# Two-layer hybrid encoder trunk on one core: trace durations in the planner, two KK and two TT tiles, independent key moves, x in four transfers

## The chip, the core and the metric

The kernel runs on one core of one Trainium2 chip. A core has a matrix engine (TensorE, PE), three engines for element-wise work (VectorE, DVE; ScalarE, ACT; GpSimd, POOL), a queue engine (SyncE, SP) that issues transfers here, and 16 DMA engines. The engines run side by side, each through its own list of instructions in order, and wait for each other by semaphores. Products go into PSUM, where one bank holds 128 x 512 float32; all else lives in SBUF. The metric is the device time of one execution in microseconds, lower is better.

## The reference

Two layers over x of 512 tokens x 1024 channels, all float32. `c` is one vector per sequence that gives six modulation vectors per layer.

```
for l in range(DEPTH):
    mod = cond @ w_ada[l] + b_ada[l];  sh1, sc1, g1, sh2, sc2, g2 = split(mod, 6)
    h = rmsnorm(x, norm1_w[l]) * (1 + sc1) + sh1
    x = x + g1 * token_mixers(h, ...)
    h = rmsnorm(x, norm2_w[l]) * (1 + sc2) + sh2
    x = x + g2 * conv_ffn(h, ...)
return rmsnorm(x, final_norm_w)

def token_mixers(h, ...):
    a_val, a_gate, q_att, k_att, v_att, q_rec, z_fwd, z_bwd, i_rec, g_rec = split(h @ w_in)
    a   = silu(layernorm(conv31(a_val * sigmoid(a_gate))))             # 256 channels
    att = mixture over 3 dilated windows of softmax attention, 6 heads # 384 channels
    rec = rmsnorm(hgrn2 forward + hgrn2 backward) * silu(g_rec)        # 384 channels, 6 heads
    return concat(a, att, rec) @ w_out

def hgrn2_gate(z, lb):
    f = lb + (1 - lb) * sigmoid(z);   k = (1 - lb) * sigmoid(-z)

def conv_ffn(h, ...):
    gate, val = split(conv3(h @ w_up));   return (gelu(gate) * val) @ w_down
```

## The kernel before

x is kept transposed, as eight tiles of 128 channels x 512 tokens, and all activations likewise. A float32 factor is split into a high part that TensorE's fast fp32r form takes whole and a low part (hi, lo), and a product is three fp32r products, high by high, high by low and low by high (`block`). Weights come from HBM in chunks of 128 rows by up to 1024 columns (tag `wr`), one chunk being one column tile over all eight row tiles; the `splitter` thread makes `wh` and `wl` of it. One column tile of w_in is thus 24 products of 512 columns into one PSUM bank (tag `g`, two banks; `m`, four, and `m2` serve all small products).

A layer's mixers begin with six column tiles at once (`FIRST`, whose h arrives tile by tile), then 22 one after the other (`REST`). As soon as a column tile is done, an `evac` thread takes it out of its bank: sigmoids for gates, high and low parts for attention's q and k, copies for values. When all tiles of a pair of heads are there, `evac` starts `rec` (the recurrence, in seven levels of small products) or `att` (attention: scores, masks, exponentials, transposes of P, products with V), and `conv` runs 31 steps on VectorE. The tiles that concern the change: `KK` and `TT` hold the two directions' key gates and decay of one pair of recurrence heads, from the read-out of the gate column Z_F to the end of that pair's `rec`. There was one of each, so `evac` of the next pair's Z_F waits for both (`"KK", "TT"` in its first yield), and its bank waits with it. Z_B of the same pair waits until Z_F has taken the tiles.

Attention's key tile needs each head's 64 rows twice, as high and low part. Head 0's tile and head 1's tile keep high and low part in different halves of the partitions, and transfers within SBUF (`shift`, line 275, issued on SP's queue) move 64 rows to the other half. For keys there were three transfers: two from tile 0 into tile 1, and one within tile 0 that overwrites rows which the other two still read, and so has to wait until both have landed.

What sets the order: nothing is scheduled on the chip. When the program is built, Python runs the threads with a model of the engines' clocks (`Clock`). Every issued operation gets a cost in us (line 160 on for the element-wise engines, `mm`, `transpose`, `dma` and `shift` for the others), and `run_threads` always continues the thread of the highest priority whose needs are met at the model's present time. The order in which operations are written is the order in which each engine runs them. So a number such as `CP` (the priority of conv, 2.5, behind recurrence's 1.0 and attention's 2.0; lower goes first) or the price of a product changes which instruction stands ahead of which. The times of the model are used for nothing else.

The start (`start`): x comes in eight transfers and then `par` (all small parameters), w_ada and w_sh tiles and the first weights, all on SP's queue. `stats` squares x on ScalarE, adds two squares on VectorE, and sums over channels on TensorE with 128x1 products, four pairs in turn; then root and reciprocal, a spread over the partitions, and `mods` makes h of it. `shifts` and `scales` make the first modulation vectors.

All operations of VectorE and ScalarE are issued by one helper and carry its line, L181; matmuls carry L284 and transposes L290. Names in the profile are tile names without buffer numbers.

Of the kernel before, what the change touches and what calls it, by code (L numbers as in the profile page):

```python
# [19 lines left out]
T = 512  # L20
# [20 lines left out]

BUFFERS = dict(wr=(4, 5), wh=(4, 4), wl=(4, 4), hx=(4, 8), qk=(4, 3), PT=(4, 4), KK=(4, 1), QQ=(4, 1), S=(4, 1),
               TT=(6, 1), ao=(2, 2), vr=(2, 2), va=(2, 1), bias=(4, 2), wa=(4, 1), tmp=(2, 5), P=(2, 2), sc=(1, 1),
               ap=(4.25, 1), acc=(2, 2), sm=(0.03125, 8), km=(2, 1), gs=(2, 3), qr=(2, 2), t2=(2, 2))
# [148 lines left out]
class Kernel:  # L193
# [79 lines left out]
    def shift(self, out, in_):  # L273

        self.nc.sync.dma_start(out=out.bitcast(F32), in_=in_.bitcast(F32))
        c = self.clk
        t = max(c.t.get("DMA", 0.0), c.t["PE"], c.written(in_) or 0.0) + size(in_) * in_.shape[0] * 4 / 350e3
        c.t["DMA"] = t
        lo, hi = span(out)
        c.w.setdefault(out.tensor.name, []).append((lo, hi, t + 2.4, "DMA"))  # L280
        c.last[out.tensor.name] = t + 2.4

    def mm(self, out, lhsT, rhs, start, stop, **kw):
        self.nc.tensor.matmul(out, lhsT=lhsT, rhs=rhs, start=start, stop=stop, **kw)  # L284
        n, m = size(out), out.shape[0]
        c = 0.009 + n * 0.000408 if rhs.dtype == F32R else n * 0.00168 * {32: 0.5, 64: 0.51}.get(m, 1.0)
        self.clk.issue("PE", c, [out], [lhsT, rhs])

    def transpose(self, out, in_):
        self.nc.tensor.transpose(out, in_, self.ident)  # L290
        self.clk.issue("PE", 0.109, [out], [in_])

# [75 lines left out]
    def splitter(self):  # L368
        for i in range(len(self.chunks)):
            more = MTAG + ["bias", "wa", "ap"] if i in self.wide else []  # L370
            yield (lambda: 0.0 if i in self.raw and i <= self.cur_chunk + (WA if i in self.wide else 3) else None,)
            t = self.raw.pop(i)
            yield (t, [["wh"] + more, 1], [["wl"] + more, 1])
            hi = self.sb([128, 1024], ["wh"] + more, F32R)[:, :t.shape[1]]
            self.copy(hi, t)
            yield (hi, DM, [["wl"] + more, 1])
            lo = self.sb([128, 1024], ["wl"] + more, F32R)[:, :t.shape[1]]
            self.v.tensor_tensor(out=lo, in0=t, in1=hi.bitcast(F32), op=ALU.subtract)
            self.give(t)
            self.wt[i] = (hi, lo)  # L380
# [49 lines left out]
    def setup(self):  # L430
# [6 lines left out]

        self.x = [one.tile([128, T], F32, name=f"x{k}") for k in range(KD)]
        self.par = one.tile([128, NPAR], F32, name="par")
# [15 lines left out]
    def bounds(self):  # L455

        g = self.par[:, P_GAM:P_GAM + 12].rearrange("p (l j) -> p l j", l=2)
        yield (self.par, lambda: self.clk.written(self.h[KD - 1]))
        lw = self.one.tile([128, 3, 6], F32, name="lw")
# [284 lines left out]
    def start(self):  # L744
# [10 lines left out]

        for k in range(KD):
            self.dma(self.x[k], a["xT"][:, k])
        self.dma(self.par, a["par"])
        for k in range(3):
            load_ada(k)  # L760
            self.loaded.add(k)
            self.load_chunk(k)
        acc = self.sb([128, T], "t2")
        halves = [slice(0, H2), slice(H2, T)]
# [19 lines left out]
        def stats():  # L784
            ps = self.pst("m")
            old = None
            for k in range(KD):
# [7 lines left out]
                v.tensor_tensor(out=sq, in0=sq, in1=old, op=ALU.add)  # L795
                self.give(old)
                yield (sq,)
                self.mean_sq(ps, [sq], slice(0, T), k == 1, k == KD - 1)
                self.give(sq)
                if k == 3:  # L800
                    for i in range(2):
                        v.tensor_copy(self.cb[:, i * 512:i * 512 + 512], cps[i].rearrange("p k c -> p (k c)"))
                    self.give(diag, *cps)
            self.preload(AF.Sqrt)
            d = yield from self.roots(ps, slice(0, T))
            self.give(ps)
            ready.append(1)
            self.spawn(scales(), 0.4)
            yield (lambda: 0.0 if len(ready) > 1 else None,)
# [8 lines left out]
        def scales():  # L818
            for k in range(KD):
                yield (lambda: 0.0 if k in self.sc else None,)  # L820
                yield (self.sc[k], self.cb, SM)
                self.ada_tile(0, 8 + k, self.sc.pop(k))
# [80 lines left out]
    def evac(self, l, n, ps):  # L903
# [51 lines left out]
        elif n >= Q_ATT:  # L955
# [16 lines left out]
            else:  # L972

                yield (ps, ["qk", 2])
                t = [self.sb([128, 2, T], "qk", F32R) for _ in range(2)]
                self.copy(t[0][:, 0], ps)
                yield (t[0][:, 0], DM)
                v.tensor_tensor(out=t[0][:, 1], in0=ps, in1=t[0][:, 0].bitcast(F32), op=ALU.subtract)
                self.give(ps)
                yield (t[0],)  # L980
                for hd in range(2):
                    self.shift(t[1][own[hd]], t[0][own[1]])
                self.shift(t[0][own[1]], t[0][own[0]])
            cur["qa" if q else "ka", p] = t
# [484 lines left out]
```

## Time and profile before

| | us |
|---|---|
| three runs | 1365.31, 1365.95, 1364.5 |
| their median | 1365.31 |
| the profiled execution's own time | 1367.1 |
| its span on the core | 1365.3 |

The profile shows one execution, whose own time is 1.8 us above the median; the span is what the profiler saw of it, from the first to the last instruction. The page gives busy time by engine, the chain of work that ended last, and groups of instructions. Windows give busy times in stretches of the span; the column PEclk there is the mean clock that TensorE was granted, as a share of full speed. Busy time of TensorE is modelled at its ends, since products are pipelined: a busy TensorE is one with work in it and not always one at its peak. A row of waits names who waited, for whose tile, total us, times, and the longest.

### The profile page before, as it was taken

How to read it: one execution, taken by the hardware profiler on the slowest of the kernel's cores; microseconds unless marked ns; L12 is line 12 of the kernel's file. 1: busy time of each engine (PE TensorE's matmuls, PEld its weight loads, DVE VectorE, ACT ScalarE, POOL GpSimd, SP SyncE). 2: the span in 40 equal slices, each digit the busy share in tenths (PEclk: the TensorE clock that was granted, in tenths of full speed). 3: DMA queues.
4: the chain of work that ended last, by engine and by line, in shares of the span. 5: the costliest groups of instructions: out<-in, count | busy, mean ns of one | idle time of the engine just before them, and what ended most of it. 6: DMA issues, size and time to landing. Idle time of an engine off the chain costs nothing.

```text
span 1365.3 us, 24377 instructions
## 1 busy us (share of the span) xinstructions
PE 1328.6 (97%) x9936; PEld 1103.7 (81%) x9936; DVE 1060.7 (78%) x1820; ACT 611.2 (45%) x1024; POOL 2.1 (0%) x16
## 2 busy tenths in 40 slices
PE   8998999999999999999999999999899999999997
PEld 7976777779988888888898786777798888888887
DVE  6898889987698999666785998888667565666666
ACT  5535548574442333233453473758445232333332
POOL 0000000000000000000000000000000000000000
PEclk9999999999999999999999999999999999999998
DMA  9645353342358787421612413114221423233221
GB/s 360 214 147 160 121 170 109 106 122 96 122 157 318 221 289 250 140 100 47 193 49 80 133 62 112 34 48 145 92 76 48 139 64 107 85 105 119 62 78 63
DMA packets 57664, 175.48 MB, mean 129 GB/s; under 512 B 6736, under 2 KB 8784, under 8 KB 57552
## 3 DMA queue, kind: packets, MB, share of 16 engines
q1 hardware_dynamic: 57552, 173.92, 39.7%
q8 instruction: 78, 1.28, 0.4%
q14 instruction: 34, 0.28, 0.1%
HBM read 165.50 MB, written 2.10 MB: 123 GB/s over the span
## 4 chain that ended last, share of the span: by engine, by line
PE 79%; DVE 13%; DMA 4%; ACT 2%; issue 2%; SPq 0%; DVEq 0%; ACTq 0%
PE m L284 52%; PE g L284 25%; DVE acc L181 2%; DMA qk<-qk 2%; DVE wl L181 2%; PE m L290 2%; DVE QQ L181 1%; DVE KK L181 1%; DVE P L181 1%; DVE tmp L181 1%; DVE TT L181 1%; DVE wa L181 1%; ACT P L181 1%; DVE x L181 1%; ACT wh L181 0%
## 5 line engine op out<-in xcount | busy, mean ns | idle before, releaser
L284 PE MATMUL g<-hx,wh 128*128 128x512 f32 (+1 forms) x1280 | 402.7, 391 | 0.5 <-DVE qr L181 0.3
L284 PE MATMUL m<-hx,wh 128*128 128x512 f32 (+1 forms) x1152 | 324.4, 365 | 1.1 <-DVE hx L181 1.1
L284 PEld LDWEIGHTS g<-hx,wh 128*128 128x128 f32 x1280 | 235.4, 189 | 49.2 <-issue 3.9
L181 DVE TENSOR_TENSOR wl<-wr,wh 128x1024 fp32r<-128x1024 f32 (+3 forms) x212 | 217.5, 1028 | 69.7 <-ACT wh L181 63.8
L181 ACT CAST wh<-wr 128x1024 fp32r<-128x1024 f32 (+3 forms) x174 | 154.8, 891 | 236.4 <-PE m L284 161.6
L284 PE MATMUL g<-hx,wl 128*128 128x512 f32 (+1 forms) x636 | 248.1, 390 | 0.0
L284 PEld LDWEIGHTS m<-hx,wh 128*128 128x128 f32 x1152 | 207.7, 189 | 36.5 <-DVE hx L181 1.7
L284 PE MATMUL m<-hx,wl 128*128 128x512 f32 (+1 forms) x584 | 211.2, 362 | 0.0
L284 PEld LDWEIGHTS g<-hx,wl 128*128 128x128 f32 x636 | 119.9, 188 | 22.6 <-issue 0.2
L284 PEld LDWEIGHTS m<-hx,wl 128*128 128x128 f32 x584 | 110.2, 189 | 16.8
L181 DVE SCALAR_TENSOR_TENSOR x<-m,mod,x 128x256 f32<-128x256 f32 (+1 forms) x112 | 66.3, 593 | 43.0 <-PE m L284 42.4
L181 DVE SCALAR_TENSOR_TENSOR acc<-ap,par,acc 128x512 f32<-128x512 f32 x120 | 89.7, 747 | 2.1
L181 DVE SCALAR_TENSOR_TENSOR tmp<-m,par,tmp 128x511 f32<-128x511 f32 x120 | 89.3, 747 | 2.0
L181 ACT ACTIVATE P<-P,sm 128x512 f32<-128x512 f32 x78 | 56.2, 723 | 49.5 <-DVE sm L181 49.3
L181 DVE CAST wh<-wr 128x1024 fp32r<-128x1024 f32 (+3 forms) x42 | 25.3, 603 | 51.8 <-PE m L284 38.3
L181 ACT ACT_TABLE_LOAD x49 | 62.9, 1283 | 4.9 <-DVE tmp L181 3.3
L181 ACT ACTIVATE tmp<-tmp 128x512 f32<-128x512 f32 x44 | 27.8, 633 | 77.2 <-DVE tmp L181 77.2
L181 ACT COPY km<-KK 128x512 f32<-128x512 f32 x30 | 20.6, 685 | 82.5 <-DVE KK L181 59.2
L181 DVE CUSTOM_DVE_ANT_0 wa<-wa,cb,par 128x1024 f32<-128x1024 f32 x40 | 51.1, 1279 | 7.1 <-DMA wa<-w_ada 7.0
L181 ACT ACTIVATE tmp<-m,par 128x512 f32<-128x512 f32 x60 | 40.6, 685 | 31.1 <-PE m L284 28.9
L181 DVE CUSTOM_DVE_ANT_0 bias<-bias,cb,par 128x1024 f32<-128x1024 f32 x39 | 49.6, 1279 | 1.6 <-DMA bias<-w_ada 1.6
L181 DVE SCALAR_TENSOR_TENSOR tmp<-g,par,tmp 128x511 f32<-128x511 f32 x56 | 41.8, 747 | 10.5 <-ACT tmp L181 9.5
(310 smaller groups left out, 2097.5 us busy)
## 6 DMA issues: line engine op xcount, KB each, us to landing
wr<-w_up SPq DMA_DIRECT2D x76, 512.0 KB, 3.5
wr<-w_in SPq DMA_DIRECT2D x44, 512.0 KB, 3.9
wa<-w_ada SPq DMA_DIRECT2D x40, 512.0 KB, 3.9
bias<-w_ada SPq DMA_DIRECT2D x39, 512.0 KB, 4.5
wr<-w_down SPq DMA_DIRECT2D x32, 320.0 KB, 3.0
wr<-w_down SPq DMA_DIRECT2D x32, 256.0 KB, 2.6
wr<-w_in SPq DMA_DIRECT2D x16, 384.0 KB, 5.7
wr<-w_up SPq DMA_DIRECT2D x16, 384.0 KB, 3.1
```

Source lines behind the costliest of these rows:

```text
L181: r = f(*a, **k)
L284: self.nc.tensor.matmul(out, lhsT=lhsT, rhs=rhs, start=start, stop=stop, **kw)
L290: self.nc.tensor.transpose(out, in_, self.ident)
```

## The change

- `KK` and `TT` get two tiles each, `wr` three instead of five.
- `CP` goes from 2.5 to 1.5: conv stands between recurrence (1.0) and attention (2.0).
- The planner's costs: fp32r products 0.0135 + n x 0.000417 us, other fp32 products by their shape, 0.1 us for each change of TensorE's tile shape (`SWITCH`), and 4.5 instead of 2.4 us from the issue of a key or query move to its landing.
- The key tile: two ScalarE copies of the bank give both heads' high parts, VectorE makes the low part, ScalarE copies it to the second tile, and then each tile has one transfer of its own, within itself.
- The start: x is one tile and comes in four transfers of two row tiles; the first 56 columns of `par` come ahead of it and the rest after the first weights; four squares are added on VectorE before they are summed on TensorE; the root's table is loaded earlier; the products of constants that `first_group` put ahead of the first real one are not in the list any more; the splitter waits for the root.

```
-BUFFERS = dict(wr=(4, 5), ..., KK=(4, 1), QQ=(4, 1), S=(4, 1),
-               TT=(6, 1), ...
+BUFFERS = dict(wr=(4, 3), ..., KK=(4, 2), QQ=(4, 1), S=(4, 1),
+               TT=(6, 2), ...
-CP = 2.5
+CP = 1.5
+SWITCH = 0.1
...
     def shift(self, out, in_):
-        c.w.setdefault(out.tensor.name, []).append((lo, hi, t + 2.4, "DMA"))
-        c.last[out.tensor.name] = t + 2.4
+        l = c.w.setdefault(out.tensor.name, [])
+        l[:] = [e for e in l if not (lo <= e[0] and e[1] <= hi)] + [(lo, hi, t + 4.5, "DMA")]
+        c.last[out.tensor.name] = c.last[in_.tensor.name] = t + 4.5
...
     def mm(self, out, lhsT, rhs, start, stop, **kw):
-        c = 0.009 + n * 0.000408 if rhs.dtype == F32R else n * 0.00168 * {32: 0.5, 64: 0.51}.get(m, 1.0)
-        self.clk.issue("PE", c, [out], [lhsT, rhs])
+        mode = (lhsT.shape[0], m)
+        if rhs.dtype == F32R:
+            c = 0.0135 + n * 0.000417
+        elif mode == (128, 128):
+            c = max(0.22 if n == 1 else 0.17, n * 0.00168 + 0.005)
+        else:
+            c = {(64, 32): 0.016, (128, 32): 0.027}.get(mode, n * 0.00086)
+        self.clk.issue("PE", c + (SWITCH if mode != self.mode else 0.0), [out], [lhsT, rhs])
+        self.mode = mode
...
     def splitter(self):
-            yield (lambda: 0.0 if i in self.raw and i <= ...
+            yield (lambda: 0.0 if self.rooted and i in self.raw
...
     def start(self):
-        for k in range(KD):
-            self.dma(self.x[k], a["xT"][:, k])
-        self.dma(self.par, a["par"])
+        self.dma(self.par[:, :P_CW], a["par"][:, :P_CW])
+        for k in range(0, KD, 2):
+            self.dma(self.xall[:, k:k + 2], a["xT"][:, k:k + 2])
         for k in range(3):
             load_ada(k)
             self.loaded.add(k)
             self.load_chunk(k)
+            if k == 0:
+                self.dma(self.par[:, P_CW:], a["par"][:, P_CW:])
...
         def stats():
                 v.tensor_tensor(out=sq, in0=sq, in1=old, op=ALU.add)
                 self.give(old)
+                if k % 4 == 1:
+                    pair = sq
+                    continue
+                yield (sq, pair)
+                v.tensor_tensor(out=sq, in0=sq, in1=pair, op=ALU.add)
+                self.give(pair)
+                if k == KD - 1:
+                    self.spawn(scales(), 0.4)
                 yield (sq,)
-                self.mean_sq(ps, [sq], slice(0, T), k == 1, k == KD - 1)
+                self.mean_sq(ps, [sq], slice(0, T), k == 3, k == KD - 1)
...
     def evac(self, l, n, ps):
                 t = [self.sb([128, 2, T], "qk", F32R) for _ in range(2)]
-                self.copy(t[0][:, 0], ps)
+                for hd in range(2):
+                    self.s.copy(t[hd][:, 0], ps)
                 yield (t[0][:, 0], DM)
                 v.tensor_tensor(out=t[0][:, 1], in0=ps, in1=t[0][:, 0].bitcast(F32), op=ALU.subtract)
                 self.give(ps)
-                yield (t[0],)
+                yield (t[0][:, 1],)
+                self.s.copy(t[1][:, 1], t[0][:, 1].bitcast(F32))
+                yield (t[1],)
                 for hd in range(2):
-                    self.shift(t[1][own[hd]], t[0][own[1]])
-                self.shift(t[0][own[1]], t[0][own[0]])
+                    self.shift(t[hd][own[1 - hd]], t[hd][own[hd]])
```

The order that the planner writes changes throughout; three places follow. In the rows `<-` stands between output and inputs, names carry the number of their buffer, and `xN` means N in a row.

The first is ScalarE in layer 0, where the gate columns of the second recurrence pair are read out of their banks (`KK<-g`, with the other sigmoid `tmp<-g`), amid the attention of the first pair (`P`). Before:

```order
L181 ACTIVATE P_226_1633,sm_228_1635<-P_226_1633,sm_227_1634 128x512
L181 CAST wh_230_1647<-wr_162_1203 128x1024
L181 ACTIVATE P_233_1658,sm_235_1660<-P_233_1658,sm_234_1659 128x512
L181 COPY st_157<-tmp_224_1618 64x3x64 x2
L181 ACT_TABLE_LOAD
L181 ACTIVATE tmp_236_1667<-g_184_1428 128x512
L181 ACTIVATE KK_237_1668<-g_184_1428 128x512
L181 ACTIVATE tmp_239_1672<-g_214_1564 128x512
L181 ACTIVATE KK_237_1668<-g_214_1564 128x512
```

With the change:

```order
L182 CAST wh_196_1494<-wr_169_1247 128x1024
L182 ACTIVATE tmp_198_1498<-g_182_1403 128x512
L182 ACTIVATE KK_199_1499<-g_182_1403 128x512
L182 COPY tmp_205_1517<-m_204_1513 128x384
L182 COPY tmp_207_1523<-m_206_1519 128x384
L182 ACT_TABLE_LOAD
L182 ACTIVATE P_208_1526,sm_210_1528<-P_208_1526,sm_209_1527 128x512
L182 ACTIVATE P_211_1531,sm_213_1533<-P_211_1531,sm_212_1532 128x512
L182 COPY tmp_217_1554<-m_216_1544 128x64
```

Before, the two read-outs stand together, behind the first pair's exponentials and a table load. Now the first of them stands ahead of those exponentials.

The second is SP's queue in layer 0, where the first key tile's moves stand (L275 before, L276 now; `qk<-tmp` is the query's). Before:

```order
L263 DMA wa_171_1281<-w_sh 128x1024
L275 DMA qk_165_1211<-tmp_166_1212 64x512 x2
L263 DMA wr_178_1347<-w_in 128x1024
L275 DMA qk_174_1289<-qk_173_1288 64x1024 x2
L275 DMA qk_173_1288<-qk_173_1288 64x1024
L263 DMA wa_182_1418<-w_ada 128x1024
L263 DMA bias_186_1432<-bias 128x896
L263 DMA bias_187_1433<-bias 128x896
```

With the change:

```order
L264 DMA wr_169_1247<-w_in 128x1024
L276 DMA qk_163_1188<-tmp_164_1189 64x512 x2
L264 DMA wa_178_1334<-w_ada 128x1024
L264 DMA wr_179_1339<-w_in 128x1024
L276 DMA qk_174_1310<-qk_174_1310 64x1024
L276 DMA qk_175_1311<-qk_175_1311 64x1024
L264 DMA bias_184_1413<-bias 128x896
L264 DMA bias_185_1414<-bias 128x896
```

Three key moves, one of which reads and writes the tile that the others read, have become two that each stay within one tile; right behind them stand the bias loads, where a wa load stood first.

The third is TensorE in the start, from the sums over channels (`m<-onesD,tmp`, 128x1) to the first product of h (`g<-hx`). Before:

```order
L284 MATMUL m_23_225<-onesD,tmp_25_228 128x1 x4
L284 MATMUL m_23_225<-onesD,tmp_29_241 128x1 x4
L284 MATMUL m_23_225<-onesD,tmp_31_252 128x1 x4
L284 MATMUL m_23_225<-onesD,tmp_33_261 128x1 x4
L284 MATMUL m_0_36_279<-PT_2_177,sc_19_202 32x128 x8
L284 MATMUL g_37_288<-tmp_35_272,onesD 128x256 x2
L284 MATMUL m_0_36_279<-mean_145,km_42_300 128x1
L284 MATMUL g_43_304<-onesC,onesD 128x128 x4
L284 MATMUL m_0_52_326<-PT_5_183,sc_19_202 32x128 x8
L284 MATMUL g_43_304<-hx_11_194,wh_40_296 128x256 x2
```

With the change:

```order
L286 MATMUL m_23_215<-onesD,tmp_27_223 128x1 x4
L286 MATMUL m_0_32_247<-PT_2_166,sc_19_192 32x128 x8
L286 MATMUL m_23_215<-onesD,tmp_31_241 128x1 x4
L286 MATMUL m_0_32_247<-mean_138,km_36_265 128x1
L286 MATMUL g_38_276<-tmp_37_271,onesD 128x256 x2
L286 MATMUL m_0_43_291<-PT_5_173,sc_19_192 32x128 x8
L286 MATMUL g_47_307<-hx_11_184,wh_39_277 128x256 x2
```

Four groups of sums have become two; the first shifts (`m<-PT,sc`) stand between them and not behind, and the products of `onesC` by `onesD` are gone.

More of the change, by code (lines that the diff above doesn't have):

```diff
@@ L39 @@
 H2 = T // 2
-BUFFERS = dict(wr=(4, 5), wh=(4, 4), wl=(4, 4), hx=(4, 8), qk=(4, 3), PT=(4, 4), KK=(4, 1), QQ=(4, 1), S=(4, 1),
-               TT=(6, 1), ao=(2, 2), vr=(2, 2), va=(2, 1), bias=(4, 2), wa=(4, 1), tmp=(2, 5), P=(2, 2), sc=(1, 1),
+BUFFERS = dict(wr=(4, 3), wh=(4, 4), wl=(4, 4), hx=(4, 8), qk=(4, 3), PT=(4, 4), KK=(4, 2), QQ=(4, 1), S=(4, 1),
+               TT=(6, 2), ao=(2, 2), vr=(2, 2), va=(2, 1), bias=(4, 2), wa=(4, 1), tmp=(2, 5), P=(2, 2), sc=(1, 1),
                ap=(4.25, 1), acc=(2, 2), sm=(0.03125, 8), km=(2, 1), gs=(2, 3), qr=(2, 2), t2=(2, 2))
@@ L285, in mm @@
         n, m = size(out), out.shape[0]
-        c = 0.009 + n * 0.000408 if rhs.dtype == F32R else n * 0.00168 * {32: 0.5, 64: 0.51}.get(m, 1.0)
-        self.clk.issue("PE", c, [out], [lhsT, rhs])
+        mode = (lhsT.shape[0], m)
[7 more added lines that the diff above has]
+        self.mode = mode
     def transpose(self, out, in_):
         self.nc.tensor.transpose(out, in_, self.ident)
-        self.clk.issue("PE", 0.109, [out], [in_])
+        self.clk.issue("PE", 0.109 + (SWITCH if self.mode != (128, 128) else 0.0), [out], [in_])
+        self.mode = (128, 128)
     def spawn(self, gen, prio, slack=0.0):
@@ L370, in splitter @@
             more = MTAG + ["bias", "wa", "ap"] if i in self.wide else []
-            yield (lambda: 0.0 if i in self.raw and i <= self.cur_chunk + (WA if i in self.wide else 3) else None,)
+            yield (lambda: 0.0 if self.rooted and i in self.raw
+                   and i <= self.cur_chunk + (WA if i in self.wide else 3) else None,)
             t = self.raw.pop(i)
@@ L436, in const @@
             return t
-        self.x = [one.tile([128, T], F32, name=f"x{k}") for k in range(KD)]
+        self.xall = one.tile([128, KD, T], F32, name="x")
+        self.x = [self.xall[:, k] for k in range(KD)]
         self.par = one.tile([128, NPAR], F32, name="par")
@@ L457, in bounds @@
         g = self.par[:, P_GAM:P_GAM + 12].rearrange("p (l j) -> p l j", l=2)
-        yield (self.par, lambda: self.clk.written(self.h[KD - 1]))
+        yield (self.par[:, P_CW:], lambda: self.clk.written(self.h[KD - 1]))
         lw = self.one.tile([128, 3, 6], F32, name="lw")
@@ L532 @@
     critical = False
+    rooted = False
+    mode = (128, 128)
     def ada_thread(self, l, order, tags, margin, every=0.0):
@@ L796, in stats @@
                 self.give(old)
+                if k % 4 == 1:
[6 more added lines that the diff above has]
+                    self.spawn(scales(), 0.4)
                 yield (sq,)
-                self.mean_sq(ps, [sq], slice(0, T), k == 1, k == KD - 1)
+                self.mean_sq(ps, [sq], slice(0, T), k == 3, k == KD - 1)
                 self.give(sq)
                 if k == 3:
+                    self.preload(AF.Sqrt)
                     for i in range(2):
@@ L803, in stats @@
                     self.give(diag, *cps)
-            self.preload(AF.Sqrt)
             d = yield from self.roots(ps, slice(0, T))
+            self.rooted = True
             self.give(ps)
             ready.append(1)
-            self.spawn(scales(), 0.4)
             yield (lambda: 0.0 if len(ready) > 1 else None,)
@@ L820, in scales @@
                 yield (lambda: 0.0 if k in self.sc else None,)
-                yield (self.sc[k], self.cb, SM)
+                yield (self.sc[k], self.cb, SM) + ((self.h[0][:, 1, :H2],) if k == 1 else ())
                 self.ada_tile(0, 8 + k, self.sc.pop(k))
```

## The prediction

> **What bounds the kernel now.** I read first the page's shares and chain of waits, then the busy times by stage, then, only in the stages where TensorE (PE) isn't always busy, its waits and the rows around them. The page's line 1 and the chain:
>
> ```profile
> PE 1328.6 (97%) x9936; PEld 1103.7 (81%) x9936; DVE 1060.7 (78%) x1820; ACT 611.2 (45%) x1024; POOL 2.1 (0%) x16
> ...
> PE 79%; DVE 13%; DMA 4%; ACT 2%; issue 2%; SPq 0%; DVEq 0%; ACTq 0%
> ```
>
> TensorE is the bound, so only what it loses can be won. The windows say where it loses (columns: stretch, its length, then busy time and count of PE, weight loads, VectorE (DVE), ScalarE (ACT), POOL, then granted clock, DMA share, GB/s). The stretches shown are the start, layer 0's mixers after their first products, with the out projection, layer 0's gated MLP, layer 1's mixers and its MLP:
>
> ```profile
> 0.00:22.00 22.00, 17.15 (x94) 15.14 (x94) 12.39 (x32) 10.24 (x19) 1.76 (x12) 1.00 0.91 334
> ...
> 63.00:312.00 249.00, 237.28 (x2688) 180.46 (x2687) 222.40 (x427) 146.38 (x268) 0.18 (x2) 0.98 0.42 130
> 312.00:735.00 423.00, 422.14 (x2210) 364.24 (x2209) 335.88 (x528) 163.77 (x252) 0.18 (x2) 1.00 0.50 164
> 735.00:968.00 233.00, 222.87 (x2578) 172.64 (x2578) 201.53 (x386) 135.93 (x240) 0.00 (x0) 0.99 0.29 86
> 968.00:1331.00 363.00, 362.66 (x1776) 307.84 (x1776) 232.91 (x327) 127.87 (x190) 0.00 (x0) 1.00 0.29 89
> ```
>
> The MLPs have nothing to give (422.14 of 423, 362.66 of 363). The mixers of layer 0 leave TensorE idle for 249.00 - 237.28 = 11.7 us, those of layer 1 for 233.00 - 222.87 = 10.1. The clock column hides a second loss, which narrower windows show:
>
> ```profile
> 131.90:138.70 6.80, 6.80 (x29) 6.36 (x29) 4.38 (x11) 5.84 (x9) 0.00 (x0) 0.50 0.45 145
> 189.90:193.30 3.40, 3.40 (x73) 2.59 (x72) 2.67 (x4) 0.00 (x0) 0.00 (x0) 0.50 0.92 310
> 961.30:964.70 3.40, 3.13 (x9) 1.98 (x11) 0.95 (x2) 1.37 (x4) 0.00 (x0) 0.50 0.38 120
> ```
>
> At clock 0.50, half of these windows is lost: 3.4, 1.7 and 1.7 us. So the mixers can give at most 11.7 + 10.1 + 6.8 = 28.6 us, 2% of the kernel. What follows asks which part of that the change reaches.
>
> **KK and TT doubled.** The rows of TensorE and then of ScalarE around 130 us:
>
> ```profile
> 126.05 0.39 PE L284 MATMUL g<-hx,wl 128*128 128x512 f32 x1
> 127.81 0.63 PE L290 MATMUL m<-ident,P 128*128 128x128 f32 x4 [1.37 <-DVE P L181]
> 130.88 0.66 PE L290 MATMUL m<-ident,P 128*128 128x128 f32 x4 [1.98 <-DVE P L181]
> 137.90 1.00 PE L284 MATMUL g<-hx,wh 128*128 128x512 f32 x2
> ...
> 133.00 0.60 ACT L181 ACTIVATE tmp<-g 128x512 f32<-128x512 f32 x1
> 133.49 0.59 ACT L181 ACTIVATE KK<-g 128x512 f32<-128x512 f32 x1
> 133.97 0.60 ACT L181 ACTIVATE tmp<-g 128x512 f32<-128x512 f32 x1
> 134.44 0.62 ACT L181 ACTIVATE KK<-g 128x512 f32<-128x512 f32 x1
> 126.40:137.90 11.50, 8.15 (x42) 7.51 (x41) 9.74 (x27) 9.21 (x16) 0.00 (x0) 0.74 0.34 104
> ```
>
> Both "g" banks hold gate columns of the second recurrence pair (Z_F+1 and Z_B+1), which ScalarE reads only at 133.0 to 135.1, when the first pair has given KK and TT back. From 126.4 to 137.9 no column product (g<-hx) is issued: TensorE lives on the attention's small transposes, which wait for VectorE. Idle is 11.50 - 8.15 = 3.35 us, and the first cold window lies here. With a second KK and TT the read-out stands right behind the product in ScalarE's order, ahead of the exponentials (first pair of order rows above). That is worth 3.35 + 3.4 = **6.75 us**; at least 0, if a bank is still held for another reason. [...]
>
> **Key moves.** A key tile was copied, its low part taken, two transfers issued, and a third that had to wait for the first two:
>
> ```profile
> 180.07 0.47 SPq L275
> 180.59 5.42 DMA qk<-qk
> 186.07 2.93 DMA qk<-qk
> SPq L275 <- DMA qk<-qk: 13.5, 3, 5.2
> SPq L275 <- DMA qk<-qk: 10.5, 3, 4.5
> PE m L284 <- DMA qk<-qk: 6.0, 5, 2.0
> DVE wa L181 <- DMA wa<-w_ada: 3.0, 1, 3.0
> DVE wa L181 <- DMA wa<-w_ada: 2.7, 1, 2.7
> 97.43 0.58 ACT L181 CAST qk<-g 128x512 fp32r<-128x512 f32 x1
> ```
>
> (The two SPq wait rows are of 60 to 312 and 735 to 972 us, the two wa rows of 63 to 130 and 130 to 200.) Now two transfers go out at once, after two more ScalarE copies. One stands ahead of the subtraction beside work that was there; the other, of the low part, is new on the path: 0.58 us. Saved per move: 0.5 of issue + 2.93 - 0.58 = 2.8 us, and the longest of TensorE's five waits is 2.0. So all **6.0 us** go (2.7 in layer 0, 3.4 in layer 1, by the same view of each stage), and the cold 1.7 at 189.9, which follows the wait that ends at 189.0. If the new order asks for the keys earlier, 3.4 remain as the low end. SP's queue was blocked for 5.2 us behind the third transfer, and the wa load queued there came late for VectorE: 3.0 + 2.7 = 5.7 us of VectorE's waits go too, in a stage where it has little to spare.
>
> **The end of layer 1's mixers.** TensorE's longest wait there:
>
> ```profile
> PE m L290 <- ACT P L181: 3.4, 1, 3.4
> 374.73 10.88 PE g L284 x48
> ```
>
> It is the last attention pair's transposes at some 960 us, with the third cold window behind. In the changed order that pair's last tiles stand about three weight chunks of the out projection, 36 products, earlier. At 10.88 / 48 = 0.227 us that is 8.2 us of cover for a wait of 3.4: 3.4 + 1.7 = **5.1 us** (0 if the pair arrives later by as much).
>
> **What it adds.** VectorE: over the program five casts and two tensor-tensors more, nearly all in layer 0's mixers.
>
> ```profile
> L181 DVE CAST wh<-wr 128x1024 fp32r<-128x1024 f32 (+3 forms) x42 | 25.3, 603 | 51.8 <-PE m L284 38.3
> 11.65 0.69 DVE L181 TENSOR_TENSOR tmp<-tmp,tmp 128x512 f32<-128x512 f32 x1 [0.65 <-ACT tmp L181]
> L181 ACT ACT_TABLE_LOAD x49 | 62.9, 1283 | 4.9 <-DVE tmp L181 3.3
> 131.70 1.28 ACT L181 ACT_TABLE_LOAD   x1
> DVE P L181 <- PE m L290: 3.0, 1, 3.0
> ```
>
> 5 x 0.603 + 2 x 0.69 = 4.4 us, so VectorE would be busy for 222.4 + 4.4 = 226.8 us of that stage. TensorE's own time there becomes 249 - 3.35 - 3.4 - 2.7 - 1.7 = 237.9. But VectorE was idle for 26.6 us, and I can name 5.7 (late loads) and 3.0 (the wait for the transposes of the stall at 130 us, last row) that go; if all else stays, it ends at 226.8 + 17.9 = 244.7. I take the middle, **241** (-8). Ends: 237.9 (-11.1), and 247.7 (-1.3) if only the late loads go.
>
> ScalarE: seven table loads more, 7 x 1.283 = 9.0 us, since exponentials and gate sigmoids now alternate, and some 7 casts more, 7 x 0.58 = 4.1. It is idle for over 95 us in either mixer stage (249 - 146.4, 233 - 135.9), so most is hidden; I count one load in the path of a read-out, **+1.5**, ends 0 and +9.0. [...]
>
> wr falls from five buffers to three. A load took 3.9 us (the page's wr<-w_in), and three buffers still start it two or more chunks ahead, of 24 products or 5.4 us each: 0, at worst +5 if one burst of loads comes late. The dearer fp32 prices, the price of a tile-mode change and conv's new rank act only through the order, which I read as it is.
>
> **The start.**
>
> ```profile
> 9.65 1.97 ACT L181 ACTIVATE tmp<-x 128x512 f32<-128x512 f32 x3 [1.01 <-DMA x<-xT]
> 11.06 3.57 PE L284 MATMUL m<-onesD,tmp 128*128 128x1 f32 x16 [0.39 <-DVE tmp L181]
> 14.56 1.10 PE L284 MATMUL m<-PT,sc 128*32 128x128 f32 x16
> 19.07 2.05 PE L284 MATMUL g<-onesC,onesD 128*128 128x128 f32 x8
> 22.08 0.58 PE L284 MATMUL g<-hx,wh 128*128 128x256 f32 x1
> ```
>
> The last sums end at 14.63; half as many are 1.8 us less, less one more addition of 0.69. But the 1.10 us of shift products stand now ahead of the last sums, and the eight filler products before the first real one are gone, so the first real ones may run at half clock. I take **-1**, ends -3 (sums and par's shorter transfer in full) and +2 (up to 3.4 us cold, 1.7, and some of the shift).
>
> **Sum**, against the profiled execution's own 1367.1 us (span 1365.3): layer 0's mixers -8, layer 1's -8.5 (3.4 + 5.1), ScalarE +1.5, start -1: -16, so 1351.1. That execution is 1.8 above the median of the runs, 1365.31; on the median's scale 1349.3, **forecast 1349**.
>
> **Rivals.** (1) VectorE sets layer 0: the gates are read early, but the recurrences behind them are VectorE's, and the stage ends at 247.7. For it: 222.4 busy of 249, more work. Against: its waits at 126 to 134 us are part of the same knot. Then -1.3 - 8.5 + 1.5 - 1 = -9.3: 1356. Chance 0.2.
> (2) A new gap, cold. In the changed order layer 0's last column products come sooner than VectorE's mixed outputs, so TensorE can run dry where the out projection begins, for VectorE's lag of 244.7 - 237.9 = 6.8 us; at half clock after it another 1.7 to 3.4 go. [...] Layer 0 then gets 249 - 237.9 - 6.8 - 3.4 = 0.9: -0.9 - 8.5 + 1.5 - 1 = -8.9, or 1356.5. Chance 0.13.
> (3) Slower: ScalarE's in-order queue. If all seven loads (9.0) stand in the chain from gate read-out through recurrence to attention, VectorE's 4.4 come on top, and the banks are held as long as before (read-outs behind loads instead of behind KK), only the waits for keys return, 6.0 + 1.7: +5.7, 1371. It decides once more than 3.3 us of loads, three of seven, lie on that chain while the banks and layer 1's end give nothing. For it: exponentials and sigmoids are interleaved in the order rows. Against: ScalarE is at 59% in that stage. Chance 0.13.
> (4) Nothing but the named waits goes wrong and the stalls I left alone (11.7 - 6.05 in layer 0, 10.1 - 6.8 in layer 1: 9 us) shrink too: 1340. Chance 0.1.
>
> **How the numbers follow.** The forecast has 0.44; its own range is 1343 to 1356. 1336 to 1365 takes in (1), (2), (4) and leaves (3) and the worst of the bounds out. About 0.2% (1362.6 to 1368.0) is what a measurement of this kernel can tell from no change. Faster: 0.42 of the forecast's 0.44, 0.16 of (1), 0.10 of (2), 0.09 of (4), 0.77 in all. Same: 0.09, the rest of these but 0.02, and 0.01 of (3). Slower: 0.12 of (3) and that 0.02, 0.14.
>
> **What would show it.** Right: no window at clock 0.50 near 130 us, sigmoid read-outs of "g" within 2 us of their products, TensorE's waits for qk below 1 us in all, L275's two transfers with no wait between them, layer 1's mixers some 8 us shorter. Wrong: a TensorE wait of over 3 us with a VectorE tile where layer 0's out projection starts (1, 2); ScalarE named by TensorE's waits for more than 5 us (3); MLP stages that change by more than 1 us, which I don't expect at all.

## The result and the profile after

| | before | changed |
|---|---|---|
| median of the runs, us | 1365.53 (1364.5 to 1365.95, 4 runs) | 1353.97 (1352.97 to 1354.47, 4 runs) |
| profiled execution's own time | 1367.1 | 1353.64 |
| span | 1365.3 | 1351.8 |

The ratio is 0.9916, 95% interval 0.9903 to 0.9929: faster by 11.6 us, 0.85%. The forecast was 1349, 16 us less than before, with a range of 1336 to 1365. So the direction and the range held, and the gain is three quarters of the one forecast. Between the two profiled executions it is 13.5 us.

The page of the changed kernel, its busy times, the chain's engines, and the rows of the table loads and of VectorE's work on the wa tiles:

```profile
PE 1321.2 (98%) x9912; PEld 1096.1 (81%) x9912; DVE 1062.1 (79%) x1824; ACT 624.8 (46%) x1041; POOL 2.1 (0%) x16
...
PE 80%; DVE 12%; ACT 5%; issue 2%; DMA 1%; SPq 0%; DVEq 0%; ACTq 0%
...
L182 ACT ACT_TABLE_LOAD x56 | 71.8, 1283 | 10.1 <-DVE tmp L182 5.6
...
L182 DVE CUSTOM_DVE_ANT_0 wa<-wa,cb,par 128x1024 f32<-128x1024 f32 x40 | 51.1, 1277 | 0.2 <-DMA wa<-w_ada 0.2
```

DMA's share of the chain fell from 4% to 1%: TensorE waits for no key move any more (its waits follow), and VectorE hardly for wa loads (0.2 us in all). The seven table loads are there, 71.8 us instead of 62.9. The windows, with the same stages as before (columns as in the prediction):

```profile
0.00:22.00 22.00, 13.54 (x78) 11.30 (x79) 13.19 (x32) 11.11 (x22) 1.89 (x14) 0.73 0.90 343
...
62.60:304.50 241.90, 234.59 (x2688) 179.21 (x2686) 224.27 (x432) 152.63 (x276) 0.00 (x0) 0.99 0.42 133
304.50:729.00 424.50, 422.56 (x2208) 364.39 (x2209) 335.15 (x528) 165.22 (x254) 0.18 (x2) 1.00 0.49 163
729.00:956.00 227.00, 222.95 (x2582) 171.09 (x2581) 202.42 (x386) 141.52 (x249) 0.00 (x0) 1.00 0.28 84
956.00:1317.00 361.00, 361.00 (x1766) 306.47 (x1765) 231.91 (x326) 126.98 (x187) 0.00 (x0) 1.00 0.30 92
```

Layer 0's mixers, from the first single column tile to the first product with the last weight chunk of the out projection (the one whose input comes last), take 241.9 us instead of 248.8; layer 1's first products and mixers together 264.2 instead of 271.0 (read from the instructions, as in the table further down). TensorE's waits in layer 0's mixers, largest first:

```profile
PE m L286 <- ACT tmp L182: 1.9, 1, 1.9
PE g L286 <- DVE x L182: 1.1, 1, 1.1
PE m L286 <- DVE sc L182: 1.0, 3, 0.6
PE m L286 <- DMA wa<-w_sh: 0.9, 1, 0.9
```

No qk among them, nor in the whole span. And the stretch that had the cold gap before is full and warm. Z_F+1 is read out at 111.7 and Z_B+1 at 121.6 us, where both were read together from 133.0 on (first the window, then ScalarE's rows):

```profile
126.40:137.90 11.50, 11.50 (x83) 9.89 (x82) 10.90 (x25) 7.63 (x14) 0.00 (x0) 1.00 0.39 131
```

```profile
111.69 0.60 ACT L182 ACTIVATE tmp<-g 128x512 f32<-128x512 f32 x1
112.18 0.60 ACT L182 ACTIVATE KK<-g 128x512 f32<-128x512 f32 x1
...
121.55 0.60 ACT L182 ACTIVATE tmp<-g 128x512 f32<-128x512 f32 x1
122.04 0.59 ACT L182 ACTIVATE KK<-g 128x512 f32<-128x512 f32 x1
```

What is new is the place that rival (2) named. TensorE runs out of column products at 245 us and starts the out projection (`g<-hx`, now with the mixers' outputs) at 256.9, 12 us later. TensorE's rows there:

```profile
244.49 0.61 PE L286 MATMUL g<-hx,wh 128*128 128x512 f32 x2
244.95 0.39 PE L286 MATMUL g<-hx,wl 128*128 128x512 f32 x1
245.50 0.75 PE L286 MATMUL m<-QQ,km 64*32 64x32 f32 x64 [0.17 <-DVE sc L182]
247.13 0.67 PE L286 MATMUL m<-wa,cT 128*32 128x128 f32 x16 [0.88 <-DMA wa<-w_sh]
...
250.29 0.38 PE L286 MATMUL m<-mean,tmp 128*128 128x1 f32 x2 [1.90 <-ACT tmp L182]
...
256.94 0.73 PE L286 MATMUL g<-hx,wh 128*128 128x512 f32 x2
```

VectorE is busy nearly all the time there (11.87 of 11.99 us), and has conv steps and a recurrence level ahead of the low part of an attention output (`hx<-ao,hx`) that the out projection needs. The windows, with a clock of 0.54 in the second, and then VectorE's rows:

```profile
244.95:256.94 11.99, 9.04 (x226) 5.54 (x224) 11.87 (x26) 6.39 (x14) 0.00 (x0) 0.86 0.59 185
252.10:255.50 3.40, 3.40 (x7) 1.79 (x6) 3.35 (x8) 0.74 (x2) 0.00 (x0) 0.54 0.43 158
```

```profile
247.21 1.53 DVE L182 SCALAR_TENSOR_TENSOR acc<-ap,par,acc 128x512 f32<-128x512 f32 x2
...
251.03 1.53 DVE L182 SCALAR_TENSOR_TENSOR acc<-ap,par,acc 128x512 f32<-128x512 f32 x2
252.47 0.69 DVE L182 TENSOR_TENSOR hx<-ao,hx 128x512 fp32r<-128x512 f32 x1
```

TensorE is idle for 2.95 of these 12 us; the rest is other products, which the list has ahead of the out projection and of which some 3.4 us run at half clock. The product at 256.94 itself waits for nothing.

So in layer 0's mixers one gap and cold stretches of 6.8 and 3.4 us went, and another gap and two cold stretches of 3.4 us came (252.4 and 262.6 us; the second is shown in the last section). Whether that made the doubled KK and TT worth anything, and what the 11.6 us are then made of, is what the experiments ask.

### The profile page after: what moved, and what is told of

Read it like the earlier page. It is cut to its first block, busy times and chain, and to the rows that moved or that the text cites. A ratio compares the mean times of both kernels' runs of the same rounds, so it can differ in the third digit from the quotient of the medians.

```text
span 1351.8 us, 24329 instructions
## 1 busy us (share of the span) xinstructions
PE 1321.2 (98%) x9912; PEld 1096.1 (81%) x9912; DVE 1062.1 (79%) x1824; ACT 624.8 (46%) x1041; POOL 2.1 (0%) x16
## 4 chain that ended last, share of the span: by engine, by line
PE 80%; DVE 12%; ACT 5%; issue 2%; DMA 1%; SPq 0%; DVEq 0%; ACTq 0%
PE m L286 50%; PE g L286 28%; DVE acc L182 2%; DVE tmp L182 2%; DVE wl L182 1%; ACT L182 1%; PE m L299 1%; ACT P L182 1%; DVE QQ L182 1%; DVE P L182 1%; DVE KK L182 1%; ACT tmp L182 1%; DVE x L182 1%; DMA PT<-w_sh 1%; DVE wa L182 1%
## 5 line engine op out<-in xcount | busy, mean ns | idle before, releaser
L286 PE MATMUL m<-hx,wh 128*128 128x512 f32 (+1 forms) x1080 | 312.2, 372 | 1.0 <-ACT hx L182 0.7
L182 DVE TENSOR_TENSOR wl<-wr,wh 128x1024 fp32r<-128x1024 f32 (+3 forms) x209 | 214.1, 1025 | 83.0 <-ACT wh L182 49.8
L182 ACT CAST wh<-wr 128x1024 fp32r<-128x1024 f32 (+3 forms) x171 | 151.9, 888 | 225.9 <-PE m L286 142.3
L286 PE MATMUL g<-hx,wl 128*128 128x512 f32 (+1 forms) x646 | 251.2, 389 | 0.0
L286 PEld LDWEIGHTS m<-hx,wh 128*128 128x128 f32 x1080 | 197.2, 189 | 36.6 <-ACT hx L182 0.9
L286 PE MATMUL m<-hx,wl 128*128 128x512 f32 (+1 forms) x556 | 204.6, 368 | 0.0
L286 PEld LDWEIGHTS m<-hx,wl 128*128 128x128 f32 x556 | 105.1, 189 | 17.2
L182 ACT ACT_TABLE_LOAD x56 | 71.8, 1283 | 10.1 <-DVE tmp L182 5.6
L182 ACT ACTIVATE tmp<-x 128x256 f32<-128x256 f32 (+1 forms) x64 | 27.9, 443 | 43.9 <-DVE x L182 40.5
```

The lines of the kernel that those rows point to most:

```text
L182: r = f(*a, **k)
```

## The experiments

All are compared with the kernel before on the same chip. Behind the changed kernel, the table's three groups of four ran on three chips, on which the kernel before has medians of 1366.16, 1365.67 and 1365.98; differences across groups carry up to half a microsecond of that. The table gives the stages of each one's profiled execution, read from the instructions of its trace: the start (to the first single column tile), from there to the first product of layer 0's out projection, from that to the first product with its last weight chunk, then layer 1 from its first column product to the same chunk. The kernels are named in the sections that follow.

| kernel | median, us | ratio to before, 95% | profiled, us | start | to out projection | out projection | both | layer 1 |
|---|---|---|---|---|---|---|---|---|
| before | 1365.53 | | 1367.1 | 63.2 | 201.7 | 47.1 | 248.8 | 271.0 |
| changed | 1353.97 | 0.9916 (0.9903 to 0.9929) | 1353.6 | 62.6 | 194.3 | 47.6 | 241.9 | 264.2 |
| a_kk1 | 1357.22 | 0.9934 (0.9921 to 0.9946) | 1358.8 | 63.2 | 201.3 | 42.9 | 244.2 | 268.6 |
| a_mv3 | 1369.18 | 1.0022 (1.0012 to 1.0031) | 1369.2 | 62.7 | 201.7 | 47.6 | 249.3 | 274.1 |
| b_kk | 1371.63 | 1.0029 (1.0017 to 1.0042) | 1371.7 | 62.6 | 191.1 | 61.1 | 252.2 | 272.3 |
| b_mv | 1356.25 | 0.9926 (0.9914 to 0.9938) | 1353.6 | 62.7 | 195.9 | 47.5 | 243.4 | 263.8 |
| b_mv24 | 1359.34 | 0.9946 (0.9934 to 0.9958) | 1358.6 | 65.0 | 196.2 | 48.9 | 245.1 | 264.0 |
| b_p45 | 1361.03 | 0.9964 (0.9950 to 0.9977) | 1366.2 | 64.1 | 200.0 | 57.9 | 257.9 | 260.4 |
| b_wr3 | 1361.81 | 0.9963 (0.9951 to 0.9975) | 1362.0 | 64.5 | 198.7 | 46.2 | 244.9 | 268.7 |
| a_fin | 1346.79 | 0.9851 (0.9836 to 0.9866) | 1349.5 | 63.2 | 183.4 | 56.4 | 239.8 | 262.8 |
| a_cv | 1348.32 | 0.9877 (0.9861 to 0.9893) | 1348.2 | 63.0 | 191.7 | 46.5 | 238.2 | 264.4 |
| kk1_cv | 1358.93 | 0.9952 (0.9940 to 0.9965) | 1359.1 | 62.9 | 201.7 | 44.3 | 246.0 | 267.5 |
| a_st | 1356.1 | 0.9936 (0.9919 to 0.9952) | 1360.1 | 67.3 | 195.4 | 46.4 | 241.8 | 266.7 |
| fin_npe | 1349.23 | 0.9881 (0.9868 to 0.9895) | 1349.2 | 61.4 | 196.5 | 43.8 | 240.3 | 265.0 |

### The two large parts, each undone and each alone

```
a_kk1 (against the changed kernel):   KK=(4, 2) -> KK=(4, 1),  TT=(6, 2) -> TT=(6, 1)
a_mv3 (against the changed kernel):   the key move's lines and shift's price as before
b_kk  (against the kernel before):    wr=(4, 3), KK=(4, 2), TT=(6, 2)
b_mv  (against the kernel before):    the changed key move's lines and shift's price of 4.5
```

> The changed kernel with one KK and one TT again (wr stays at three). Theory A (each freed wait is worth its own size): the second pair's gate read-out waits for the first recurrence again, no column product for some 10 us near 120 to 135 us, a window at clock 0.50 there: 1354 + 6.75 = 1361 us. Theory B (VectorE sets layer 0's mixers, the banks don't matter): the out projection of layer 0 starts when it did, 1354 to 1356 us.

> The changed kernel with the three chained key moves and their old price of 2.4 us in the planner. Theory A: TensorE's waits for qk come back, 5 to 7 us in all, and one cold window of 1.7 us: 1360 to 1362 us. Theory B (VectorE and the order set the time, the wait is hidden or turns into another): 1353 to 1356 us.

> The kernel before with two KK, two TT and three wr alone. Theory A: the gap at 126 to 138 us and its cold window go, 1365.5 - 6.75 = 1359 us, qk waits of 6 us stay. Theory B: what layer 0's TensorE wins is given back where the out projection starts, since VectorE's work is the same: 1363 to 1366 us.

> The kernel before with the two independent key moves alone (and their price of 4.5 us in the planner). Theory A: qk waits of 6.0 us and the cold window at 190 us (1.7) go, late wa loads too: 1365.5 - 7 = 1358 to 1359 us. Theory B: the tile is there sooner but layer 0 goes on at VectorE's pace: only layer 1's 3.4 us, 1362 us.

With `shift`'s price goes the planner's note that a move holds its source tile until it has landed. Of the four results only a_kk1's lies between its two theories. The other three lie outside both: b_mv is some 2 us faster than theory A's range, a_mv3 and b_kk are slower than either theory allowed.

The key moves with their price are worth more than my 7.7 us, and the doubled tiles less than my 6.75. Moves alone bring 9.9 us; with everything but them the kernel is 3 us slower than before, so taking them away costs 15. KK and TT alone, with three wr, make it 5.5 us slower (eight runs, three of them at 1366.8 to 1368.5 and five at 1371.6 to 1372.3), and taking them away from the changed kernel costs 3.3, with intervals that overlap. The moves alone and the whole change can't be told apart either (0.9926 and 0.9916, with intervals that overlap for the most part): all the rest together added nothing that these runs can show.

With the moves chained, TensorE's waits for them are larger than before (9.5 us against 6.0), and a recurrence copy that comes late joins them:

```profile
PE m L285 <- DMA qk<-qk: 9.5, 5, 3.0
PE m L285 <- ACT S L182: 5.1, 1, 5.1
```

In b_mv the two moves go out in one stretch, with the bias loads right behind them on SP's queue, where before a third move waited 5.2 us:

```profile
181.74 1.11 SPq L275 DMA_DIRECT2D qk<-qk  x2
182.90 1.62 SPq L263 DMA_DIRECT2D bias<-bias  x2
```

Yet b_mv keeps the gap that I had set down as 6.75 us, at 120 to 134 us, idle for 4.4 us and with a clock of 0.78 (in a window's row TensorE's busy time stands first, behind the length). With one KK and TT in the changed kernel the clock is lower still, 0.56, with 4.1 us idle:

```profile
120.00:134.00 14.00, 9.61 (x57) 8.17 (x55) 12.68 (x31) 10.42 (x21) 0.00 (x0) 0.78 0.47 137
```

```profile
122.00:136.00 14.00, 9.89 (x37) 7.59 (x38) 12.65 (x32) 9.97 (x22) 0.00 (x0) 0.56 0.33 114
```

and neither kernel is slower at the end of layer 0 by anything like it. The table shows why. In a_kk1 the out projection starts 7.0 us later than in the changed kernel (201.3 against 194.3), but then takes 4.7 us less (42.9 against 47.6). In b_kk it is the other way round: it starts 10.6 us earlier than before and takes 14.0 longer. Whatever TensorE gains ahead of the out projection waits behind it for the third recurrence pair and attention. In b_kk these waits stand at its end, on VectorE's and ScalarE's last outputs:

```profile
306.38 0.63 PE L290 MATMUL m<-ident,tmp 128*128 128x128 f32 x4 [2.12 <-DVE tmp L181]
309.16 1.31 PE L284 MATMUL m<-hx,KK 128*128 128x256 f32 x2 [2.15 <-ACT hx L181]
312.80 1.31 PE L284 MATMUL m<-hx,wa 128*128 128x256 f32 x2 [2.11 <-ACT hx L181]
```

In the profiled executions the doubling is worth 2.3 us in layer 0's mixers (244.2 against 241.9) and 4.4 in layer 1 (268.6 against 264.2), where I had given it no term.

### The transfer or its price; and three wr alone

```
b_mv24: the changed key move's lines, shift's price still 2.4
b_p45:  three chained key moves, shift's price 4.5
b_wr3:  wr=(4, 5) -> wr=(4, 3)
```

> The kernel before with the two independent key moves, and the planner's old price of 2.4 us for them. The moves alone with their price gave 1356.3. Theory A (the transfers themselves: no third one behind two): most of it stays, 1357 to 1360 us, qk waits under 2 us. Theory P (the planner's price does it: at 2.4 us the scores are put where the key hasn't landed): 1362 to 1366 us, qk waits of 4 us or more.

> The kernel before with its three chained key moves, priced at 4.5 instead of 2.4 us in the planner. Theory A: the chain of 7 to 9 us is still longer than the price covers: qk waits of 2 to 5 us stay, 1363 to 1366 us. Theory P: the scores stand later and the waits are filled, 1356 to 1360 us.

> The kernel before with three wr buffers instead of five, nothing else. KK, TT and three wr together gave 1371.6. Theory A (my price of nothing for wr holds; the loss comes from the doubled KK and TT): 1364 to 1367 us. Theory W (three buffers make weights late): 1369 to 1372 us, and TensorE or VectorE waits for wr or wl.

The transfers alone give 6.3 us, within what theory A said, and TensorE's waits for qk are nearly gone without any change of price:

```profile
PE m L284 <- DMA qk<-qk: 0.8, 1, 0.8
```

The price alone gives 4.6 us, more than theory A allowed and less than theory P asked; TensorE's waits for qk fall to 2.2 us, though the moves are still chained. Its runs spread from 1358.4 to 1366.2, and the profiled one is the slowest of them, so its row in the table is of little use. Together they give 9.9, about the sum, so the price adds 3 to 5 us. In layer 1 the transfers alone give all of it (264.0 against 271.0).

Three wr buffers are not what made b_kk slow: alone they make the kernel 3.9 us faster, which neither theory expected. TensorE waits for no weights there beyond 0.5 us, and its wait of 3.4 us at the end of layer 1's mixers is gone (1.0 us for `P` in all). No row shows a load that comes sooner with fewer buffers, so I read the gain as one of order, which no run shows by itself: the planner lets loader and splitter go at other times, and everything behind them is written in another order. If so, a change of order with no purpose moves this kernel by some 4 us, and below that size a single knob's effect says little of its mechanism. The loss of b_kk against b_wr3, 9 to 10 us, is then that of KK and TT, or of the order that came with them; the runs don't separate these two.

### Is it VectorE that hands the gain back?

```
a_cv:    conv, changed kernel:  for i in range(1, CW)  ->  range(1, CW if l else 16)
kk1_cv:  the same in a_kk1
a_fin:   changed kernel:  yield from self.finish_mixed(...)  ->  self.spawn(self.finish_mixed(...), 0.5)   (three places)
fin_npe: a_fin with NPE = 5 -> 9
```

> The changed kernel with conv of layer 0 cut to 16 of its 31 taps (taps 16 to 30 are left out: part of the computation is gone, to take 30 steps of 0.748 us, 22 us, off VectorE). Theory V (VectorE sets layer 0's mixers in the changed kernel): TensorE's own time, about 10 us less than now, becomes the bound: 1342 to 1346 us. Theory T (TensorE and its waits set it): 1351 to 1354 us.

> The changed kernel with one KK and one TT, and the same 15 taps of layer 0's conv left out. Beside the run with two of each and the same cut it gives what the doubling is worth when VectorE has room; with the whole conv it was 3.2 us. Theory V: 6 to 10 us more than that run (the gap of 6.75 us can no longer be handed back), 1350 to 1354 us. Theory T: the same 3 us or less.

> The changed kernel, with the last step of each mixer (high and low part of its output, finish_mixed) as a thread of its own at priority 0.5, ahead of recurrence, conv and attention. In the changed kernel the out projection of layer 0 starts 12 us behind the last column product, with four conv steps and a recurrence level ahead of the low part it needs. Theory O (VectorE's order there holds TensorE up): 3 to 5 us less, 1349 to 1351 us. Theory V (VectorE's total work up to there is the bound, so what goes first only moves the wait): 1353 to 1355 us.

> The kernel of the run a_fin (mixers' last step as its own thread), with nine instead of five of layer 0's later modulation tiles computed on TensorE: four VectorE operations of 1.28 us less, four groups of small products of some 0.7 us more. Theory V: VectorE's 5 us less win 2 to 4 us, 1343 to 1345 us. Theory T: TensorE's 3 us more cost that much, 1349 to 1350 us.

With 22 us less for VectorE in layer 0, the doubled KK and TT are worth 1358.93 - 1348.32 = 10.6 us, with intervals far apart; with the whole conv they were worth 3.3. Theory V had 6 to 10 for this difference, theory T 3 or less. In the profiled executions the change sits in layer 0's mixers, where the doubling gives 7.8 us (246.0 against 238.2) and gave 2.3; in layer 1, whose conv is whole in all four, it gives 3.1 and gave 4.4. So the gap costs about what its rows show, but TensorE keeps the gain only where VectorE has room. The 7 us between 10.6 and 3.3 are more than the 4 us by which three wr moved the kernel, though not by much. The stretch of the gap, in kk1_cv and then in a_cv:

```profile
122.00:136.00 14.00, 9.95 (x38) 7.69 (x37) 12.59 (x32) 9.97 (x23) 0.00 (x0) 0.56 0.35 114
```

```profile
122.00:136.00 14.00, 14.00 (x84) 12.21 (x83) 13.51 (x33) 11.25 (x22) 0.00 (x0) 1.00 0.46 147
```

But a_cv itself gains only 5.7 us, between the two theories, and kk1_cv gains nothing against a_kk1. So VectorE's total is not the bound by itself. fin_npe says the same: four VectorE operations less, and it is 2.4 us slower than a_fin, not faster. Its time is the one that theory T gave, but its rows don't show TensorE's extra work as the cause: layer 0's mixers take 240.3 us against 239.8, and layer 1, which the edit leaves alone, 265.0 against 262.8. My reading is that what counts is what stands first on VectorE where TensorE waits. a_fin is the test of it: its one edit puts the mixers' outputs ahead of conv, recurrence and attention (in both layers, and the rest of the order moves with it), and the out projection follows the last column product at once, 1.26 us after it began instead of 12:

```profile
245.35 0.39 PE L287 MATMUL g<-hx,wl 128*128 128x512 f32 x1
245.93 0.75 PE L287 MATMUL m<-QQ,km 64*32 64x32 f32 x64 [0.20 <-DVE sc L183]
246.61 1.06 PE L287 MATMUL g<-hx,wh 128*128 128x512 f32 x2
```

It is the fastest kernel here, 1346.8, 7.2 us below the changed one, more than theory O's 3 to 5, and with an interval clear of it. Of the 10.9 us by which its out projection starts earlier, 8.8 are given back in it (56.4 against 47.6), as in the other kernels; its layer 1 is 1.4 us shorter. Its profiled execution is the slowest of its runs, so the table shows too little of its gain, and where the rest of the 7.2 us lies stays open.

### The start

```
a_st: x in eight transfers, par in one behind them, squares in pairs, Sqrt's table, splitter and scales as before
```

> The changed kernel with the old start: x in eight transfers, par in one behind them, squares summed in pairs, the filler products as the planner's old rules put them. My term: the new start is worth 1 us, so 1355 us, within 1352 to 1357 (the bounds of -3 and +2). Rival: the order behind it shifts, and the time moves by more than 3 us either way without the start's own rows showing it.

The median is 2.1 us above the changed kernel's, within my bounds, and the intervals overlap, so the start's worth isn't settled; its runs spread from 1353.4 to 1360.1, more than the effect. Its profiled execution, one of the two slowest, has the long start in its own rows: the first single column tile stands at 67.3 us instead of 62.6. The seven profiled kernels with the old start have it at 62.6 to 67.3 us, 64.2 in the mean, the seven with the new one at 61.4 to 63.2, 62.7 in the mean, which speaks for about 1.5 us.

In the changed kernel the shifts do stand ahead of the last sums, the first product of h starts 2.1 us earlier (19.99 against 22.08), and it does so cold:

```profile
12.28 1.10 PE L286 MATMUL m<-PT,sc 128*32 128x128 f32 x16 [1.25 <-DMA PT<-w_sh]
13.31 1.87 PE L286 MATMUL m<-onesD,tmp 128*128 128x1 f32 x8
...
19.99 1.10 PE L286 MATMUL g<-hx,wh 128*128 128x256 f32 x2 [0.49 <-ACT hx L182]
```

```profile
20.00:23.00 3.00, 3.00 (x12) 2.77 (x13) 2.97 (x7) 1.75 (x5) 0.00 (x0) 0.50 1.02 405
23.00:26.40 3.40, 3.40 (x37) 3.07 (x37) 3.37 (x8) 0.88 (x3) 0.00 (x0) 0.90 1.04 410
```

A clock of 0.50 up to 23.0 and for a fifth of the next window (mean 0.90), 3.7 us in all, costs 1.8 of the 2.1. The old start was cold too, though the prediction's row of 0 to 22 us gives 1.00: the profile's record of the clock begins only at 22.7 us there, and the row counts what lies before as full. The lengths of the products tell it. Sixteen small products take 1.10 us in both starts, and 0.67 at 247.13 in the changed kernel, where the clock is full; two products of h take 0.40 from 22.79 on in the kernel before, and 0.63 at 21.11 in the changed one (two rows of before, then one of changed):

```profile
21.05 1.10 PE L284 MATMUL m<-PT,sc 128*32 128x128 f32 x16
22.79 0.40 PE L284 MATMUL g<-hx,wh 128*128 128x256 f32 x2
...
21.11 0.63 PE L286 MATMUL g<-hx,wh 128*128 128x256 f32 x2
```

From 22.08 to 22.7 the old start lost 0.3 us in this way. So 2.1 - 1.8 + 0.3 = 0.6 us is left, and that is what the first single column tile shows (62.6 against 63.2).

## Why the prediction was right, and where it was wrong

**Bound and stages.** Right. The mixers gave 6.9 us (forecast 8) and 6.8 (forecast 8.5). What follows layer 1's mixers moved by 0.3 us. Layer 0's MLP became 1.1 us longer, just past the 1 us that I had named as a sign of being wrong: TensorE waits there 1.6 us for `wl`, where it waited 0.7 before.

**Key moves.** Right in mechanism, too small in size. I took 6.0 us of waits and 1.7 of clock, 7.7 in all; the transfers alone (b_mv24) bring 6.3, and with their price the moves bring 9.9. The step that failed is the price of 4.5 us in the planner, for which the sum has no term: of the other prices I said that they "act only through the order, which I read as it is", and this one I left out. It brings 3 to 5 us, I think by putting other products ahead of the scores, since the waits for chained moves fall to 2.2 us with it. The late wa loads behind the third move went as I said (VectorE's waits for them in layer 0's mixers are 6.5 us before, 1.8 in b_mv24 and 0.2 in b_mv); what that was worth, no run separates.

**KK and TT.** The gap, its cause and its disappearance are as described. That the cold 3.4 us belong to the gap and go with it was my estimate from its rows; the stretch from 126.4 to 137.9 us has a clock of 0.74 in the kernel before and of 1.00 in the changed one. As a term of this kernel's sum, 6.75 us failed: it is 3.3 when undone, not clear of zero, and by the profiles 2.3 in layer 0's mixers, where I had put it (7.8 there with conv cut). The step was to take the whole of it off TensorE's side (237.9) and to answer VectorE's side (244.7) only by the middle of the two, 241. The stage came out at 241.9, within a microsecond, but that is luck: the middle has no mechanism behind it, and one term in it was three times too large. The doubling's share in layer 1 (4.4 us by the profiles) has no term at all. Rival (1) had the mechanism that the experiments point to, with all of layer 0's gain lost; most of the gain was kept, and b_mv, where the banks are held as long as before, has 5.4 of its 6.9 us from the moves.

**The new gap (rival 2).** It came, where it was named, with VectorE busy and a cold stretch in it and another behind it. Against "a wait of over 3 us with a VectorE tile", the trace shows three shorter ones, the longest of 1.9 us on a ScalarE copy. It did not take layer 0's gain. The 3.4 us at half clock in its sum were my estimate, and the kernel before shows no cold stretch at this place; the changed one shows two of 3.4 us at half clock, which lost 1.7 us each. (Its sum gives 1356.4, not 1356.5.)

**The end of layer 1's mixers.** The wait of 3.4 us and its cold window are gone, and the stage is 6.8 us shorter. My cause, the pair's earlier place in the new order, isn't needed for it: b_mv24, with the old planner's prices and priorities, has the same 7 us, and there the pair's last transposes stand behind all products of the out projection's first half, as in the kernel before. In the changed kernel 16 of these products follow them, not the 36 that I had read.

**ScalarE (rival 3).** It didn't happen. Seven loads were added and no single wait of TensorE for ScalarE exceeds 1.9 us. They sum to 5.1 us, just past the 5 that I had named as its sign, but were 4.6 before. Behind the load at 131.70 us in the kernel before no further pause shows: it ends at 132.98, and ScalarE's next operation starts at 133.00. The two kernels that came out slower than before, a_mv3 and b_kk, both have chained moves beside doubled tiles.

**wr at 0.** No late weights show, as I said, but three buffers alone win 3.9 us, outside my 0 to +5; I put that down to the order.

**The start.** Forecast -1, and some -0.6 to -2 by the profiles and medians. The half clock, which I had counted as a cost of the new start, was in the old one too, up to 22.7 us; the new one loses more to it only because its products of h come earlier.

**The sum.** 16 us forecast, 13.5 between the profiled executions, 11.6 between medians. The total was nearer than its parts, and that is luck: the moves were too small by some 2 us and KK with TT too large by some 3, of opposite sign.

## What to carry to other kernels

A stall that is removed on one engine is worth its length only if the next thing that this engine waits for isn't set by another engine's order (the doubled tiles brought 10.6 us with VectorE's conv cut and 3.3 with it whole): follow the gain to the next meeting point (here the out projection) and see who arrives last. There, look first at what stands in front of the awaited operation in that engine's queue; moving each mixer's short last step ahead brought 7.2 us, more than the doubled buffers did. And where a planner writes the order, measure how much a knob without purpose moves the time, since smaller effects of one knob prove little.

## What the runs showed of the hardware

In the mixers of the kernel before, TensorE's clock falls to 0.50 three times. The 3.4 us ahead of the three cold windows hold 1.42, 1.35 and 0.26 us of work at a clock of 1.00, and the first two have no idle of more than 2.1 us within (1.98 us up to 130.9, 2.05 up to 189.05):

```profile
128.50:131.90 3.40, 1.42 (x11) 1.02 (x9) 3.33 (x9) 2.03 (x6) 0.00 (x0) 1.00 0.26 105
186.50:189.90 3.40, 1.35 (x7) 0.75 (x5) 1.44 (x4) 1.59 (x3) 0.00 (x0) 1.00 0.79 220
957.90:961.30 3.40, 0.26 (x2) 0.00 (x0) 2.41 (x5) 1.46 (x3) 0.00 (x0) 1.00 0.39 116
```

In the changed kernel the clock falls at 252.4 us, and the 3.4 us up to 252.1 hold 1.81 us of work:

```profile
248.70:252.10 3.40, 1.81 (x70) 1.62 (x71) 3.37 (x8) 1.52 (x4) 0.00 (x0) 1.00 0.97 291
```

There the clock halves once more at 262.6 us, with hardly an idle ahead of it: TensorE is busy for 3.31 of the 3.40 us from 257.6 on, and from 259.4 its work is 16 products of one column (128x1), then 64 of 64x64 and four transposes:

```profile
257.60:261.00 3.40, 3.31 (x23) 2.66 (x21) 2.10 (x7) 2.90 (x9) 0.00 (x0) 1.00 0.00 0
261.50:264.90 3.40, 3.40 (x76) 2.93 (x74) 2.51 (x6) 3.31 (x4) 0.00 (x0) 0.67 0.02 5
```

What in this work brings the clock down, no run here shows: none varied it alone.

The same program on the same chip spread by up to 7.8 us (b_p45, 1358.4 to 1366.2) where the kernel before spread by 4.4 to 5.1, so these runs don't settle effects of 2 to 3 us.
